# RWKV-7 recurrence on one core: outputs of the chunk behind in one burst with the solve

## The chip, the cores and the metric

The kernel runs on one NeuronCore of a Trainium2 chip. The metric is the device time of one execution in microseconds, as the median of several runs. TensorE (PE, with its weight loads PEld), VectorE (DVE), ScalarE (ACT), GpSimd (POOL) and SyncE (SP, which issues nearly all transfers) run side by side and wait for each other by semaphores.

## The reference

One layer of a hybrid trunk over 512 frames and 16 meta tokens, width 2048. After RMSNorm one projection of 8,320 columns feeds two groups. Group A (16 heads of 64) is an RWKV-7 recurrence, group B a gated convolution of width 3. Both are gated, joined, sent through one output projection, added to the residual and normalised. The recurrence is what the change touches:

```python
def step(S, inp):
    r_t, w_t, k_t, v_t, kk_t, b_t = inp
    sa = jnp.einsum('bhvk,bhk->bhv', S, kk_t)
    S = (S * w_t[:, :, None, :] - sa[..., None] * b_t[:, :, None, :]
         + v_t[..., None] * k_t[:, :, None, :])
    y_t = jnp.einsum('bhvk,bhk->bhv', S, r_t)
    return S, y_t
```

It runs over the 16 meta frames and then over 512 real ones; the head outputs `y` are normalised per head (mean and variance over 64), scaled, gated and projected. All inputs and the output are float32.

## The kernel before

The frames are worked on in chunks of 64 (`CH`): chunk 0 holds the meta tokens, chunks 1 to 8 the real frames (`NCH` = 9). The 16 heads are 8 pairs; a pair fills 128 partitions, one head in each half. `prepare` and `invert` run once per pair or two pairs and write, per chunk, the operands of the recurrence to DRAM: decayed r and k products, the triangular inverse (`O_X`), the values (`vd`) and the decayed b and k (`bd`).

Then `recur` goes through the chunks in order. For one chunk c it does this on PE, with small float32 matmuls, 64 by 64 (the update: 128 rows by 64):

- **rz** (L1102, 32 matmuls, 16 in chunk 0): state times the kk operand, plus the part from the values inside the chunk. ACT negates it into `pn` (L1110).
- **solve** (L1119, 16 matmuls): the inverse times `pn`, into the second half of the same two PSUM banks. ACT and DVE copy it into `uv` (L1122, L1123).
- **zs** (L1131, 16 matmuls): `bw` times `uv`, the update of the state, in the bank of tag `misc`; DVE adds it to the state `st` and multiplies by the decay (L1152, L1153).
- **zy** (L1141, 48 matmuls): the chunk's outputs, from the old state, `vn` and `uv`, half in the bank of tag `ser`, half in the first half of rz's first bank. `norm` (L1160 to L1194) normalises them on DVE, ACT and POOL, and stores them to `yd` some time later.

The profile counts two matmuls, each with a weight load, for each of these float32 matmuls.

PE's order is the order of the program (a manual schedule); the other engines' queues are ordered ahead of time by a planner with priorities (`ahead()` raises one). Between the steps `fill(ns)` issues matmuls of the big input projection (L353 and L368, tiles `ps_C`, `ps_h`, `ps_B`, `ps_gc` in this stretch) until their planned time has reached ns; the projection is one generator, so the amount of filler is fixed by the sum of the budgets: `p` 2900 after rz, `u` 2900 after the solve, `s` 4200 plus `mid` 1000 at the end of the chunk. The weights of this filler arrive as `wr` by SP's queue (L159, 512 KB each, three buffers) and are split by ACT (L151) and DVE (L152) into high and low parts (`w`, six buffers). A scheduled store (`later`) leaves when the filler's planned time has come.

`load_chunk` loads one 192 KB tile `ct` for each pair, `load_shared` loads `vn`, `uv` (its other half) and `bw`. All of these have two buffers. Pairs 0 to 3 of chunk c + 2 and the shared tiles are requested at the end of chunk c, pairs 4 to 7 of chunk c + 1 after rz of chunk c.

After the last chunk the rest of the projection runs, and then the output projection (L1383).

Of the kernel before, what the change touches and what calls it, by code (L numbers as in the profile page):

```python
# [9 lines left out]
F32 = mybir.dt.float32  # L10
# [3 lines left out]
ALU = mybir.AluOpType  # L14
# [4 lines left out]
P = 128  # L19
# [5 lines left out]
CH = 64  # L25
NCH = SEQ // CH + 1
LP = NCH * CH
NPAIR = 8
# [9 lines left out]
OPW = 6 * CH  # L38
O_AR, O_KK, O_BR, O_X = 0, 128, 256, 320
# [50 lines left out]
def hymba_kernel(ctx: ExitStack, tc: tile.TileContext, xt, xtok, front, w_in, w_out, pv, lup, cst, msk, gf, out):  # L90
    nc = tc.nc
# [91 lines left out]
    pi = ph1.enter_context(tc.tile_pool(name="pi", bufs=1, space=PSUM))  # L183
# [66 lines left out]
    o = 0  # L250
# [62 lines left out]
    with tc.issue_after(head):  # L313
        nc.vector.tensor_scalar(
            out=omm, in0=pvt[:, V_MU : V_MU + 33], scalar1=-1.0, scalar2=1.0, op0=ALU.mult, op1=ALU.add
# [299 lines left out]
    def fill(ns):  # L615
        while ns > 0:
            seen = len(ready)
            t = step()
            if t is None:
                return  # L620
            ns -= t
            if len(ready) > seen:
                ns += FW["evac"]
# [23 lines left out]
    def ahead():  # L647
        return tc.high_priority(offset=AHEAD)
# [409 lines left out]

    def load_chunk(ch, c, pairs, ops):
        for i in pairs:  # L1060
            t = ch.tile([P, OPW], F32, tag=f"ct{i}", name=f"ct{i}_{c}", bufs=2)
            nc.sync.dma_start(t, spot(i, 0, P, c, 1, 1, 0, OPW))
            ops[c, i] = t

    def load_shared(ch, c, ops):
        n = CH * NPAIR * CH
        vn = ch.tile([P, NPAIR, CH], F32, tag="vn", name=f"vn{c}", bufs=2)
        uv = ch.tile([P, 2, NPAIR, CH], F32, tag="uv", name=f"uv{c}", bufs=2)
        bw = ch.tile([P, NPAIR, 2, CH], F32, tag="bw", name=f"bw{c}", bufs=2)
        nc.sync.dma_start(vn, vd[2 * c * n : (2 * c + 2) * n].rearrange("(s j d) -> s j d", j=NPAIR, d=CH))  # L1070
        for h, hs, ho in heads:
            if c < NCH - 1:
                nc.sync.dma_start(
                    uv[ho, h], vd[(2 * c + h) * n : (2 * c + h + 1) * n].rearrange("(s j d) -> s j d", j=NPAIR, d=CH)
                )
                nc.sync.dma_start(
                    bw[hs].rearrange("p j h d -> p (j h d)"),
                    bass.AP(
                        tensor=bd.tensor, offset=bd.offset + (h * (NCH - 1) + c) * CH * NPAIR * P,
                        ap=[[NPAIR * P, CH], [1, NPAIR * P]],  # L1080
                    ),
                )
        ops[c] = vn, uv, bw


    def recur(ch):
        ops = {}
        for c in range(2):
            load_chunk(ch, c, range(NPAIR), ops)
            load_shared(ch, c, ops)  # L1090
        st = None
        for c in range(NCH):
            last = c == NCH - 1
            vn, uv, bw = ops[c]
            z = [pz.tile([P, 2, 4, CH], F32, tag="tz", name=f"rz{c}_{e}") for e in range(2)]
            for k in range(4):
                for part in range(0 if c else 1, 2):
                    for e in range(2):
                        t = ops[c, 2 * k + e]
                        o = O_KK if part else O_AR  # L1100
                        for h, hs, ho in heads:
                            nc.tensor.matmul(  # L1102
                                z[e][ho if e else hs, 0, k], t[hs, o : o + CH],
                                vn[hs, 4 * e + k] if part else st[hs, 4 * e + k],
                                start=(part == 0 or c == 0), stop=(part == 1),
                            )
            pn = ch.tile([P, 2, 4, CH], F32, tag="pn", name=f"pn{c}", bufs=2)
            with ahead():
                for e in range(2):
                    nc.scalar.activation(pn[:, e], z[e][:, 0], AF.Copy, scale=-1.0)  # L1110
            if c and not last:
                load_chunk(ch, c + 1, range(4, NPAIR), ops)
            fill(FW["p"])
            for k in range(4):
                for e in range(2):
                    t = ops[c, 2 * k + e]
                    for h, hs, ho in heads:
                        m = ho if e else hs
                        nc.tensor.matmul(z[e][hs, 1, k], t[m, O_X : O_X + CH], pn[m, e, k], start=True, stop=True)  # L1119
            with ahead():  # L1120
                for h, hs, ho in heads:
                    nc.scalar.copy(uv[hs, h, 0:4], z[0][hs, 1])  # L1122
                    nc.vector.tensor_copy(uv[hs, h, 4:8], z[1][hs, 1])  # L1123
            fill(FW["u"])
            if not last:
                zs = pi.tile([P, NPAIR, CH], F32, tag="misc", name=f"zs{c}")
                for k in range(4):
                    for e in range(2):
                        j = 4 * e + k
                        for h, hs, ho in heads:  # L1130
                            nc.tensor.matmul(zs[hs, j], bw[:, j, h], uv[:, h, j], start=True, stop=True)  # L1131
            if c:
                zy = (pi.tile([P, 4, CH], F32, tag="ser", name=f"zy{c}"), z[0][:, 0])
                for k in range(4):
                    for n in range(3):
                        for e in range(2):
                            t, j = ops[c, 2 * k + e], 4 * e + k
                            for h, hs, ho in heads:
                                o = (O_AR + CH, O_KK + CH, O_BR)[n]
                                x = (st[hs, j], vn[hs, j], uv[hs, h, j])[n]  # L1140
                                nc.tensor.matmul(  # L1141
                                    zy[e][hs if e else ho, k], t[hs, o : o + CH], x, start=(n == 0), stop=(n == 2)
                                )
            if c + 2 < NCH:
                load_chunk(ch, c + 2, range(0, 4), ops)
                load_shared(ch, c + 2, ops)
            if not last:
                new = ch.tile([P, NPAIR, CH], F32, tag="st", name=f"st{c}", bufs=2)
                scale = dd[:, c].unsqueeze(2).to_broadcast([P, NPAIR, CH])
                with ahead():  # L1150
                    if c:
                        nc.vector.tensor_tensor(out=new, in0=zs, in1=st, op=ALU.add)  # L1152
                    nc.vector.tensor_tensor(out=new, in0=new if c else zs, in1=scale, op=ALU.mult)  # L1153
                st = new
            if c:
                norm(ch, zy, c)
            fill(FW["s"] + FW["mid"])


    def norm(ch, zs, c):  # L1160
        nv = ch.tile([P, 4, NPAIR], F32, tag="nv", name=f"nv{c}", bufs=2)
        yc = ch.tile([P, NPAIR, CH], F32, tag="yc", name=f"yc{c}", bufs=2)
        yt = ch.tile([P, NPAIR * CH], F32, tag="yt", name=f"yt{c}", bufs=2)

        def spread(j):
            return nv[:, j].unsqueeze(2).to_broadcast([P, NPAIR, CH])

        for z, j in zip(zs, (slice(0, 4), slice(4, NPAIR))):
            nc.vector.tensor_reduce(out=nv[:, 0, j], in_=z, op=ALU.add, axis=AX.X)
            nc.vector.scalar_tensor_tensor(  # L1170
                out=yc[:, j], in0=spread(0)[:, j], scalar=-1.0 / CH, in1=z, op0=ALU.mult, op1=ALU.add
            )
        yq = yt.rearrange("p (j s) -> p j s", s=CH)
        nc.scalar.activation(yq, yc, AF.Square)
        nc.vector.tensor_reduce(out=nv[:, 1], in_=yq, op=ALU.add, axis=AX.X)
        nc.gpsimd.tensor_scalar(
            out=nv[:, 2], in0=nv[:, 1], scalar1=1.0 / CH, scalar2=LNX_EPS, op0=ALU.mult, op1=ALU.add
        )
        rsqrt(nv[:, 3], nv[:, 2])
        nc.vector.tensor_tensor(out=yc, in0=yc, in1=spread(3), op=ALU.mult)  # L1180
        nc.vector.transpose(yt, yc.rearrange("p j s -> p (j s)"))

        def put():
            for b in range(4):
                nc.sync.dma_start(
                    bass.AP(
                        tensor=yd.tensor,
                        offset=yd.offset + (b // 2) * NPAIR * CH * SEQ + (c - 1) * CH + 32 * (b % 2),
                        ap=[[SEQ, 32], [32 * SEQ, 2 * NPAIR], [1, 32]],
                    ),  # L1190
                    yt[32 * b : 32 * b + 32].rearrange("p (t s) -> p t s", s=32),
                )

        later(10500, put)  # L1194
# [497 lines left out]
```

## Time and profile before

| | us |
|---|---|
| median of 3 runs | 991.01 |
| lowest, highest | 990.09, 991.07 |
| profiled execution | 991.42 |
| span of its instructions | 989.6 |
| PE busy | 980.0 |
| PEld busy | 908.2 |
| DVE busy | 706.9 |
| ACT busy | 391.2 |
| POOL busy | 126.8 |

The recurrence lies between about 621 us (first rz) and 767 us (last normalisation begun). In the profile, times are from the span's start. L followed by a number is a line of the kernel before. In a row such as `670.98 0.66 ACT L1110 ACTIVATE pn<-rz ... x2 [1.11 <-PE rz L1102]` stand the start, the length, engine, line, operation, output and inputs, shapes, count, and in brackets how long the engine was idle before it and what ended that. The chain of waits gives the work that ended last, step by step: start, length, engine, tile, line and count. A row of a table of windows gives for each engine the busy time and the number of instructions, then the clock share, the share of the DMA engines and GB/s. A row of DMA queues gives packets, megabytes and the share of the 16 DMA engines' time; q1 carries the data, q8 and q14 carry instructions. The clock of TensorE was 0.999 of full speed over the span.

### The profile page before, as it was taken

To read this page: it belongs to the slowest core of one execution; us is meant where nothing else is said; L and a number is where in the kernel's file an instruction comes from. 1 tells how busy PE (TensorE), PEld (TensorE's weight loads), DVE (VectorE), ACT (ScalarE), POOL (GpSimd) and SP (SyncE) were. 2 spreads that over 40 slices of the span, in tenths; PEclk is the share of its full clock that TensorE was granted. 3 is DMA by queue.
4 is the path that set the end of the run, shared out by engine and by line. 5 is a ranking of instruction groups with operands and counts; after the bars stand their busy time and mean duration, and the time that the engine had idled before them with its cause. 6 is when DMAs were issued, how large, how long until landed. Compare 5 with 4: busy or idle time off the path is not lost.

```text
span 989.6 us, 23389 instructions
## 1 busy us (share of the span) xinstructions
PE 980.0 (99%) x9511; PEld 908.2 (92%) x9511; DVE 706.9 (71%) x1415; ACT 391.2 (40%) x730; POOL 126.8 (13%) x241
## 2 busy tenths in 40 slices
PE   9999999999999999999999999999999999999996
PEld 9999999999998999998999998889888898888885
DVE  7777966578775779653778654365756697997897
ACT  7553432343322534322434323232332335556464
POOL 0110302112010121010111010011211102001001
PEclk9999999999999999999999999999999999999999
DMA  9436577246674284853275856999896697797654
GB/s 339 143 91 150 144 199 167 86 128 148 157 179 165 91 195 116 209 153 114 86 181 124 203 143 193 277 252 260 223 264 171 179 289 187 187 320 180 160 128 170
DMA packets 205531, 176.89 MB, mean 179 GB/s; under 512 B 138544, under 2 KB 168048, under 8 KB 205040
## 3 DMA queue, kind: packets, MB, share of 16 engines
q1 hardware_dynamic: 202976, 166.76, 60.4%
q0 software_dynamic: 2304, 8.39, 4.9%
q8 instruction: 74, 1.21, 0.5%
q14 instruction: 33, 0.27, 0.1%
q10 hardware_dynamic: 144, 0.26, 0.1%
HBM read 139.02 MB, written 36.35 MB: 177 GB/s over the span
## 4 chain that ended last, share of the span: by engine, by line
PE 96%; DVE 2%; issue 1%; DMA 0%; ACT 0%; POOL 0%; POOLq 0%; DVEq 0%; ACTq 0%
PE ps_v L353 9%; PE ps_h L353 9%; PE ps_C L353 9%; PE ps_g L353 9%; PE ps_B L368 9%; PE ps_gc L368 9%; PE ps_k L353 8%; PE ps_r L353 8%; PE M L1383 7%; PE P L1383 3%; PE Q L1383 2%; PE g L755 2%; PE ps_k L368 1%; PE ps_r L368 1%; PE ps_lora L368 1%; PE zy L1141 1%
## 5 line engine op out<-in xcount | busy, mean ns | idle before, releaser
L151 ACT CAST w<-wr 128x512 fp32r<-128x512 f32 x252 | 154.1, 619 | 293.9 <-PE ps_C L353 47.4
L152 DVE TENSOR_TENSOR w<-wr,w 128x512 fp32r<-128x512 f32 x252 | 174.7, 704 | 121.0 <-ACT w L151 119.8
L353 PE MATMUL ps_v<-xh,w 128*128 128x256 f32 (+2 forms) x512 | 84.0, 284 | 0.0
L368 PE MATMUL ps_B<-xh,w 128*128 128x512 f32 x256 | 83.4, 394 | 0.0
L353 PE MATMUL ps_h<-xh,w 128*128 128x256 f32 (+2 forms) x512 | 81.6, 281 | 0.0
L353 PE MATMUL ps_g<-xh,w 128*128 128x256 f32 (+2 forms) x512 | 81.4, 281 | 0.0
L368 PE MATMUL ps_gc<-xh,w 128*128 128x512 f32 x256 | 81.1, 392 | 0.0
L353 PE MATMUL ps_C<-xh,w 128*128 128x256 f32 (+2 forms) x512 | 80.8, 280 | 0.0
L353 PEld LDWEIGHTS ps_v<-xh,w 128*128 128x128 f32 x512 | 73.9, 188 | 0.3
L353 PE MATMUL ps_k<-xh,w 128*128 128x256 f32 (+1 forms) x448 | 73.4, 285 | 0.0
L353 PE MATMUL ps_r<-xh,w 128*128 128x256 f32 (+1 forms) x448 | 72.5, 280 | 0.0
L353 PEld LDWEIGHTS ps_g<-xh,w 128*128 128x128 f32 x512 | 71.9, 189 | 0.6 <-issue 0.2
L353 PEld LDWEIGHTS ps_h<-xh,w 128*128 128x128 f32 x512 | 72.1, 189 | 0.3
L353 PEld LDWEIGHTS ps_C<-xh,w 128*128 128x128 f32 x512 | 71.8, 189 | 0.2
L353 PEld LDWEIGHTS ps_k<-xh,w 128*128 128x128 f32 x448 | 64.7, 188 | 0.4
L353 PEld LDWEIGHTS ps_r<-xh,w 128*128 128x128 f32 x448 | 63.5, 189 | 0.4 <-issue 0.2
L353 PE MATMUL ps_h<-xl,w 128*128 128x256 f32 x256 | 57.3, 281 | 0.0
L368 PEld LDWEIGHTS ps_gc<-xh,w 128*128 128x128 f32 x256 | 47.8, 188 | 10.0
L368 PEld LDWEIGHTS ps_B<-xh,w 128*128 128x128 f32 x256 | 47.9, 188 | 9.7
L353 PE MATMUL ps_C<-xl,w 128*128 128x256 f32 x256 | 56.2, 280 | 0.0
L353 PE MATMUL ps_v<-xl,w 128*128 128x256 f32 x256 | 55.8, 278 | 0.0
L353 PE MATMUL ps_g<-xl,w 128*128 128x256 f32 x256 | 55.4, 278 | 0.0
(383 smaller groups left out, 2143.5 us busy)
## 6 DMA issues: line engine op xcount, KB each, us to landing
wr<-in_w_in_dram SPq DMA_DIRECT2D x126, 512.0 KB
ct<-opd SPq DMA_DIRECT2D x72, 192.0 KB
wo<-in_w_out_dram SPq DMA_DIRECT2D x24, 512.0 KB
x<-in_w_out_dram POOLq DMA_DIRECT2D x16, 512.0 KB, 5.9
opd<-ar SPq DMA_DIRECT2D x8, 576.0 KB
opd<-gt SPq DMA_DIRECT2D x16, 288.0 KB
bd<-bt SPq DMA_DIRECT2D x64, 64.0 KB
bw<-bd SPq DMA_DIRECT2D x16, 256.0 KB
```

Source lines behind the costliest of these rows:

```text
L151: nc.scalar.copy(hi, rq)
L152: low[q] = eng.tensor_tensor(out=lo, in0=rq, in1=hi.bitcast(F32), op=ALU.subtract).ins
L353: nc.tensor.matmul(ps[r][:, 0 : b - a], ww[:, k * P : (k + 1) * P], xx[:, kt, a:b], start=(kt == 0 and n == 0), stop=(kt == KT - 1 and n = ...
L368: nc.tensor.matmul(ps[r], ww[:, w], xx[:, kt, a:b], start=(kt == 0 and n == 0), stop=(kt == KT - 1 and n == 2))
L755: nc.tensor.matmul(z[h][:, c - c0], bk[hs, c, h : h + 2, :].rearrange("p a s -> p (a s)"), ar[hs, c].rearrange("p a s -> p (a s)"), start= ...
L1141: nc.tensor.matmul(zy[e][hs if e else ho, k], t[hs, o : o + CH], x, start=(n == 0), stop=(n == 2))
L1383: nc.tensor.matmul(bank[s], left(prod, jj, m, s), w, start=(jj == 0 and n == 0), stop=(jj == 7 and n == 2))
```

## The change

- `outputs(c)` is a function of its own now. In chunks 2 to 8 the outputs of chunk c - 1 are computed between rz and the solve of chunk c, in place of the filler `p`; the last chunk computes its own outputs as well, after the filler `u`.
- The `p` filler of chunks 1 to 7 is added at the end of the chunk (`s` + `mid` + `p`).
- After the solve and the filler `u` stands the update of the state alone. It is written to the first halves of rz's banks and added to the state in two halves, and then multiplied by the decay in one operation.
- The outputs of chunks 1 to 7 use the banks of tags `ser` and `misc`; `norm` of chunk c - 1 follows the solve of chunk c.
- `ct` of pairs 0 to 3, `vn` and `uv` get a third buffer, since chunk c - 1 is still read in chunk c. Pairs 4 to 7 of chunk c + 1 are requested behind the solve of chunk c instead of behind rz.

```diff
-            t = ch.tile([P, OPW], F32, tag=f"ct{i}", name=f"ct{i}_{c}", bufs=2)
+            t = ch.tile([P, OPW], F32, tag=f"ct{i}", name=f"ct{i}_{c}", bufs=3 if i < 4 else 2)
...
-        vn = ch.tile([P, NPAIR, CH], F32, tag="vn", name=f"vn{c}", bufs=2)
-        uv = ch.tile([P, 2, NPAIR, CH], F32, tag="uv", name=f"uv{c}", bufs=2)
+        vn = ch.tile([P, NPAIR, CH], F32, tag="vn", name=f"vn{c}", bufs=3)
+        uv = ch.tile([P, 2, NPAIR, CH], F32, tag="uv", name=f"uv{c}", bufs=3)
...
-        st = None
+        st, states = None, {}
+
+        def outputs(c, zy=None):
+            vn, uv, bw = ops[c]
+            zy = zy or [pi.tile([P, 4, CH], F32, tag=tag, name=f"zy{c}_{tag}") for tag in ("ser", "misc")]
+            for k in range(4):
+                for n in range(3):
+                    for e in range(2):
+                        t, j = ops[c, 2 * k + e], 4 * e + k
+                        for h, hs, ho in heads:
+                            o = (O_AR + CH, O_KK + CH, O_BR)[n]
+                            x = (states[c][hs, j], vn[hs, j], uv[hs, h, j])[n]
+                            nc.tensor.matmul(
+                                zy[e][hs if e else ho, k], t[hs, o : o + CH], x, start=(n == 0), stop=(n == 2)
+                            )
+            return zy
...
-            if c and not last:
-                load_chunk(ch, c + 1, range(4, NPAIR), ops)
-            fill(FW["p"])
+            zy = outputs(c - 1) if c > 1 else fill(FW["p"])
...
+            if c and not last:
+                load_chunk(ch, c + 1, range(4, NPAIR), ops)
+            if zy:
+                norm(ch, zy, c - 1)
             fill(FW["u"])
-            if not last:
-                zs = pi.tile([P, NPAIR, CH], F32, tag="misc", name=f"zs{c}")
...
+            if last:
+                norm(ch, outputs(c, [z[e][:, 0] for e in range(2)]), c)
+                fill(FW["s"] + FW["mid"])
+                break
+            for k in range(4):
+                for e in range(2):
+                    j = 4 * e + k
+                    for h, hs, ho in heads:
+                        nc.tensor.matmul(z[e][hs, 0, k], bw[:, j, h], uv[:, h, j], start=True, stop=True)
             if c + 2 < NCH:
                 load_chunk(ch, c + 2, range(0, 4), ops)
                 load_shared(ch, c + 2, ops)
...
+            with ahead():
+                for e in range(2):
+                    part = slice(4 * e, 4 * e + 4)
                     if c:
-                        nc.vector.tensor_tensor(out=new, in0=zs, in1=st, op=ALU.add)
-                    nc.vector.tensor_tensor(out=new, in0=new if c else zs, in1=scale, op=ALU.mult)
-                st = new
-            if c:
-                norm(ch, zy, c)
-            fill(FW["s"] + FW["mid"])
+                        nc.vector.tensor_tensor(out=new[:, part], in0=z[e][:, 0], in1=st[:, part], op=ALU.add)
+                    else:
+                        nc.vector.tensor_tensor(out=new[:, part], in0=z[e][:, 0], in1=scale[:, part], op=ALU.mult)
+                if c:
+                    nc.vector.tensor_tensor(out=new, in0=new, in1=scale, op=ALU.mult)
+            st = new
+            states[c + 1] = st
+            fill(FW["s"] + FW["mid"] + (FW["p"] if c else 0))
```

More of the change, by code (lines that the diff above doesn't have):

```diff
@@ L1123, in recur @@
                     nc.vector.tensor_copy(uv[hs, h, 4:8], z[1][hs, 1])
+            if c and not last:
+                load_chunk(ch, c + 1, range(4, NPAIR), ops)
+            if zy:
+                norm(ch, zy, c - 1)
             fill(FW["u"])
-            if not last:
-                zs = pi.tile([P, NPAIR, CH], F32, tag="misc", name=f"zs{c}")
[L1127 to L1131, printed above, removed]
-            if c:
[L1133 to L1143, printed above, removed]
+            if last:
[7 more added lines that the diff above has]
+                        nc.tensor.matmul(z[e][hs, 0, k], bw[:, j, h], uv[:, h, j], start=True, stop=True)
             if c + 2 < NCH:
@@ L1146, in recur @@
                 load_shared(ch, c + 2, ops)
[L1147 to L1150, printed above, removed]
-                    if c:
-                        nc.vector.tensor_tensor(out=new, in0=zs, in1=st, op=ALU.add)
-                    nc.vector.tensor_tensor(out=new, in0=new if c else zs, in1=scale, op=ALU.mult)
-                st = new
-            if c:
-                norm(ch, zy, c)
-            fill(FW["s"] + FW["mid"])
+            new = ch.tile([P, NPAIR, CH], F32, tag="st", name=f"st{c}", bufs=2)
+            scale = dd[:, c].unsqueeze(2).to_broadcast([P, NPAIR, CH])
+            with ahead():
+                for e in range(2):
+                    part = slice(4 * e, 4 * e + 4)
+                    if c:
+                        nc.vector.tensor_tensor(out=new[:, part], in0=z[e][:, 0], in1=st[:, part], op=ALU.add)
[6 more added lines that the diff above has]
+            fill(FW["s"] + FW["mid"] + (FW["p"] if c else 0))
     def norm(ch, zs, c):
```

## The prediction

> **What bounds the kernel now.** I read the page first (span, busy shares, queues, chain), then the chain of waits and the stages inside the recurrence, then ACT, DVE and the DMA queues there.
>
> ```profile
> span 989.6 us, 23389 instructions
> PE 980.0 (99%) x9511; PEld 908.2 (92%) x9511; DVE 706.9 (71%) x1415; ACT 391.2 (40%) x730; POOL 126.8 (13%) x241
> q8 instruction: 74, 1.21, 0.5%
> 621.00:755.00 134.00, 133.72 (x2323) 118.81 (x2322) 75.50 (x138) 37.83 (x77) 20.98 (x22) 1.00 0.90 252
> ```
>
> TensorE sets the end: PE is busy for 980.0 of 989.6 us. In the window of the recurrence (columns: PE, PEld, DVE, ACT, POOL, clock, DMA share, GB/s) it is idle for 0.28 of 134 us, at clock 1.00. Projection matmuls fill every gap of the recurrence, so shorter latency alone is worth nothing. Only what PE itself spends counts, and any new wait of PE. The DMA engines are 0.90 busy there, near their own limit. The profiled execution took 991.42 us, 1.8 more than its span and 0.4 above the median of 991.01.
>
> One chunk in the chain of waits (start, length, what, count):
>
> ```profile
> 669.86 1.09 PE rz L1102 x64
> 670.95 3.35 PE ps_C L353 x27
> 674.30 0.62 PE rz L1119 x32
> 674.92 3.35 PE ps_C L353 x27
> 678.27 1.08 PE zs L1131 x32
> 679.35 0.20 PE zy L1141 x2
> ...
> 680.85 0.04 PE zy L1141 x2
> 680.91 1.63 PE ps_C L353 x12
> 682.54 4.17 PE ps_h L353 x36
> 686.72 1.09 PE rz L1102 x64
> ```
>
> From rz to rz the period is 16.86 us. Each start of a run of small matmuls costs something of its own. Matmuls of rz and of the solve (L1119) have one shape: 64 take 1.09 and 32 take 0.62, so one takes 0.47/32 = 0.0147 us and the entry into the burst 0.15. The outputs (zy, from 679.35 to 680.91) are 96 matmuls: 96 x 0.0147 = 1.41 in 1.56, so the step from zs (128 rows) to zy (64 rows) costs 0.15 as well. Filler without a burst before it goes at 4.17/36 = 0.116 each; 27 of them would take 3.14 and take 3.35 behind a burst, so the way back costs 0.2.
>
> **The change part by part.**
>
> *Bursts.* The matmuls and the filler are the same in number: fill asks 11,000 ns per chunk before and, over the loop, after. Chunks 2 to 8 run rz, outputs of the chunk behind and solve as one burst: seven times the solve's entry (0.15) and one way back to filler (0.2) go. At chunks 1 to 7 no zy follows zs: seven times 0.15. Sum: 7 x 0.35 + 7 x 0.15 = 3.5 us off PE. Outputs of chunk 8 stay a burst of their own.
>
> *Does the solve wait for pn?* The filler between rz and solve was its cover; now it is the outputs.
>
> ```profile
> 670.98 0.66 ACT L1110 ACTIVATE pn<-rz 128x256 f32<-128x256 f32 x2 [1.11 <-PE rz L1102]
> 679.40 0.69 DVE L1152 TENSOR_TENSOR st<-zs,st 128x512 f32<-128x512 f32 x1 [0.63 <-PE zs L1131]
> 680.13 0.69 DVE L1153 TENSOR_TENSOR st<-st,dd 128x512 f32<-128x512 f32 x1
> 691.82 1.14 ACT L151 CAST w<-wr 128x512 fp32r<-128x512 f32 x2 [3.32 <-DMA wr<-in_w_in_dram]
> 692.87 0.75 ACT L1122 COPY uv<-rz 64x256 f32<-64x256 f32 x2
> ```
>
> ```profile
> 691.16 0.62 PE rz L1119 x32
> ```
>
> Both pn copies end at 671.64, 0.69 after rz; the outputs take 1.41. So the wait is nothing as long as ACT is free, with 0.7 to spare where 3.4 us of filler stood. If ACT is not free, the rest is PE idle. The last rows show the danger: casts held up by a late weight transfer ran until 692.87, and the uv copies that were due when the solve ended (691.78) began 1.1 late, hidden by filler. I take nothing, and keep 0 to 2 for it.
>
> *State update.* Two adds on halves instead of one, some 0.1 to 0.2 us more on DVE. After zs now come 8.1 us of filler instead of 1.56 of outputs and 5.2; st took 1.4 us. Cost nothing; without the filler it would be the full 1.6. zs lands in rz's banks, which pn has left by then; norm starts later by some 8 us of filler, its next reader (the next outputs) being a chunk away. Cost nothing.
>
> *Transfers.* The bytes are the same. Loads of ct 4 to 7 for the next chunk moved behind the solve and now wait for the outputs in the burst; behind them on SP's queue stand the yd stores, the weight loads and the next chunk's loads. They have 3.1 + 1.2 + 8.7 = 13 us until rz needs them. The third buffers let ct 0 to 3, vn and uv start at that burst too instead of behind the update. Nothing is queued on POOL by the change, whose part in norm moves with it. Cost nothing on PE, from 0 to 2 by way of the late casts above.
>
> *Instructions.* Here lies what the burst may cost. PE and PEld make 19,022 instructions for 74 packets of q8 (16 KB each): 257 per packet, so PE's program arrives in blocks of 256. PE's only stop in the recurrence, in the chain of waits, with q8 before and in it:
>
> ```profile
> 748.31 5.80 PE ps_h L353 x48
> 754.11 0.60 PE rz L1102 x26
> 754.72 0.82 issue
> 755.53 0.81 PE rz L1102 x35
> ```
>
> Queues of two windows, 742.5 to 753.2 and 753.2 to 754.4:
>
> ```profile
> q1 hardware_dynamic: 2396, 2.60, 85.1%
> ```
>
> ```profile
> q1 hardware_dynamic: 76, 0.13, 29.7%
> q8 instruction: 1, 0.02, 5.2%
> ```
>
> For 10.7 us no packet came, then one, and 1.1 to 1.3 us after it PE went on. That is a stop for want of instructions. From the first burst (621.08) to the stop PE executed 2323 + 2322 instructions and 32 waits, 4,677 = 18 x 256 + 69. So a block starts 69 instructions after the first burst, and each 256 on. Counted back from the stop, blocks start near 670.33 and 720.60:
>
> ```profile
> 670.31:755.00 84.69, 84.41 (x1543) 76.33 (x1536) 50.32 (x94) 23.70 (x48) 14.86 (x16) 1.00 0.86 244
> ```
>
> (3,079, less some 30 still running at the edge, and 20 waits, for 12 x 256 = 3,072.) Their packets, in windows 670.3 to 674.3, 674.3 to 675.5, and 720.7 to 721.5, 721.5 to 722.6:
>
> ```profile
> q1 hardware_dynamic: 456, 1.12, 102.8%
> ```
>
> ```profile
> q1 hardware_dynamic: 315, 0.43, 101.6%
> q8 instruction: 1, 0.02, 5.5%
> ```
>
> ```profile
> q1 hardware_dynamic: 64, 0.17, 98.3%
> ```
>
> ```profile
> q1 hardware_dynamic: 68, 0.20, 75.8%
> q8 instruction: 1, 0.02, 5.4%
> ```
>
> So as PE begins one block, the next is asked for and its packet comes 1 to 4 us later among busy queues (at least 4.9 at the stop, whose block began in the burst that ended at 748.31). A packet takes about 1.0, and 1.3 more until PE runs. A block lasts 7 us with filler in it, which hides this. The largest burst so far, zs with zy, holds 256 instructions in 2.64 us.
>
> The new burst holds 192 matmuls, 384 instructions, in 0.15 + 192 x 0.0147 = 2.97 us: a block that lies wholly in it lasts 128 x 0.0147 = 1.9. With two instructions per matmul, four or five waits per chunk and the filler counts that fill's budget gives, the burst of chunk 2 begins 778 instructions after the first burst; a block starts 837 after it, 59 into the burst, the next 315 into it. For chunk 4 it is 77 and 333, for chunk 7 97 and 353. In chunks 3, 5, 6 and 8 the start that counts lies so (211 to 255) that filler and zs help, about 5 us and more. So three stops are due, each of delay + 1.0 + 1.3 - 1.9 = delay + 0.4. Bounds: delay 0, with an instruction queue of some depth running ahead, gives nothing; delay 4, 4.4. Which delay? By the DMA shares:
>
> ```profile
> 666.00:669.80 3.80, 3.80 (x34) 3.63 (x32) 2.73 (x5) 2.22 (x4) 0.97 (x2) 1.00 0.99 300
> 676.50:680.80 4.30, 4.30 (x144) 4.08 (x142) 2.48 (x4) 0.62 (x1) 0.00 (x0) 1.00 0.46 115
> 728.50:731.40 2.90, 2.90 (x132) 2.63 (x130) 2.75 (x5) 0.63 (x1) 0.00 (x0) 1.00 0.36 61
> ```
>
> The queues are full ahead of rz (0.99) and run dry (0.46, 0.36) just where the outputs are about to free buffers. After the change the outputs free them in the merged burst, so that is where the dry stretch should move. I take the short delay, 1.2: 3 x 1.6 = 4.8 us. The stop of 754.72 (0.8) goes, since its block then ends elsewhere.
>
> [...]
>
> Sum: 991.42 - 3.5 - 0.8 + 4.8 = 991.9 us.
>
> **The rivals.**
>
> *Instructions come in time* (faster): the bursts' 3.5 and the 0.8 stay, 991.42 - 4.3 = 987.1. For it: one stop in the whole recurrence is thin evidence, my count of instructions may be off by a few tens, and dry queues may deliver within 0.5 us. Against it: the count of 256 fits, and no packet quoted at a burst's block came in under 0.9 us. With two of three stops at 0.6 it would still be 988.3.
>
> *Instructions come late* (slower): the delay is as at 670.33 where queues were full. At 2.7, the middle of 1 and 4 and a little over, each stop costs 3.1: 991.42 - 4.3 + 9.3 = 996.4. From a delay of 1.6 at each stop (3 x 2.0 = 6.0, 993.1) it is slower than before by over 0.2%. For it: DMA 0.90 busy. Against it: the dry stretch.
>
> *pn is late* (slower only with the stops): a cast that waits for weights stands ahead of pn on ACT. One or two such, of 1.1 less 0.7 up to 2 us each, give 0.4 to 4 on the sum, 992.3 to 996. Against it, in the view of waits (total, times, longest), ACT stood ready and waited for rz eight times:
>
> ```profile
> ACT pn L1110 <- PE rz L1102: 14.4, 8, 4.1
> ```
>
> *Nothing gained*: entries and ways back are not a cost of switching but of matmuls that queue anyway. Then 991.4 + 4.8 - 0.8 = 995.4. Against it: L1119's 0.62 and rz's 1.09 split the same way in each chunk.
>
> **How the numbers follow.** 0.2% is 2.0 us, about what a measurement of this kernel can tell from no change: 989.0 to 993.0. Stops of 0.8 to 1.9 each, 989.5 to 992.9: 0.40, the likeliest, 991.9. Instructions in time or nearly: 0.30, 987 to 989. Late instructions, late pn or no gain: 0.30, 993 to 998; above 996 lies 0.1, under 987.0 little. Range 987.0 to 996.0.
>
> **What would show it.** PE's matmul lines keep their counts. The chain shows rz x64, zy and rz x32 of the solve without filler between, some 2.97 us, and no zy behind zs. A gap named issue, or a break in PE's rows, about 313 to 355 instructions into the bursts of chunks 2, 4 and 7, with a q8 packet just before its end, is the stop; none there, and the time near 987, proves the first rival. A solve that follows an ACT cast held by a weight transfer proves pn late. The prediction is wrong most likely in the delay, or in where blocks fall.

## The result, and the profile after

The change made the kernel slower: 999.22 us as the median (996.05 to 1000.95), against 990.98 of the kernel before on the same chip, a ratio of 1.0086 with a 95% interval of 1.0072 to 1.0100. The prediction was 991.9, and the result lies above its range. The execution that was profiled is the shortest of the four, 996.05; what the longer ones add is shown by a second profile further down.

Span and TensorE of the page, and the window of the recurrence (the same stretch and columns as before):

```profile
span 994.3 us, 23392 instructions
PE 977.5 (98%) x9511; PEld 907.8 (91%) x9511; DVE 706.2 (71%) x1423; ACT 391.4 (39%) x730; POOL 128.3 (13%) x241
621.00:755.00 134.00, 126.39 (x2153) 113.55 (x2144) 71.47 (x137) 37.40 (x75) 19.04 (x20) 0.99 0.86 246
```

TensorE has the same 9511 matmuls. It was idle for 0.28 us of this window before; now it is idle for 7.61 us. The chain of waits shows where, and what a burst is without a stop (chunk 3 first, then the ends of the bursts of chunks 2, 4 and 7; the runs of outputs are left out):

```profile
672.66 1.09 PE rz L1118 x64
...
675.15 0.47 PE rz L1133 x32
675.62 3.35 PE ps_C L353 x27
```

```profile
656.23 2.38 issue
658.61 0.21 PE zy_misc L1103
...
691.48 1.19 issue
692.67 0.58 PE rz L1133 x21
```

```profile
741.14 0.33 PE rz L1133 x19
741.47 4.04 issue
745.51 0.50 PE rz L1133 x13
746.01 4.14 PE ps_C L353 x21
750.16 0.71 PE ps_h L353 x6
```

The burst of chunk 3 takes 675.62 - 672.66 = 2.96 us: rz, the outputs and the solve (L1133), whose 32 matmuls now take 0.47 and not 0.62. In chunks 2, 4 and 7 a gap without any named releaser stands inside the burst. From matmul to matmul the three gaps are 2.59, 1.41 and 4.26 us, 8.26 in all. The instruction behind each is number 12,993, 14,273 and 16,065 of PE's matmuls, weight loads and waits, counted from 0; the stop of the kernel before lay at 16,577. All four leave 193 when divided by 256. They are starts of blocks, 317, 337 and 359 instructions into their bursts (the prediction had 315, 333 and 353).

In the stop of chunk 7, the block ahead of it began at 739.34. The data and instruction queues in 739.4 to 743.2 and in 743.2 to 744.4:

```profile
q1 hardware_dynamic: 601, 1.24, 95.6%
```

```profile
q1 hardware_dynamic: 319, 0.44, 101.0%
q8 instruction: 1, 0.02, 5.2%
```

For 3.9 us only data came; then the packet of instructions, and 2.27 us after its start PE went on, at 745.51. In chunks 2 and 4 the packet began 2.10 and 0.80 us after the block, and PE went on 2.38 and 2.48 after that.

The time adds up. From the first rz to the end of the outputs of chunk 8, bursts took 37.24 us in 27 pieces before and take 42.47 in 20 now. Without the stops (a gap of 1.04 before, 8.26 now) that is 36.20 and 34.21. What the filler takes beyond the rates of a pure run fell from 5.33 to 3.78, once the slow clock behind the longest stop, 1.54, is set apart. So the change saved 1.99 + 1.55 = 3.5 us, as meant, and 1.04 with the old stop, and paid 8.26 and 1.54: 989.6 - 3.5 - 1.0 + 8.3 + 1.5 = 994.9, 0.6 over the span of 994.3; the first rz began 0.6 earlier. (The expectations below have 3.6, with 0.97 counted for the old stop.)

### The profile page after: what moved, and what is told of

Read it like the earlier page. It is cut to its first block, busy times and chain, and to the rows that moved or that the text cites. A ratio compares the mean times of both kernels' runs of the same rounds, so it can differ in the third digit from the quotient of the medians.

```text
span 994.3 us, 23392 instructions
## 1 busy us (share of the span) xinstructions
PE 977.5 (98%) x9511; PEld 907.8 (91%) x9511; DVE 706.2 (71%) x1423; ACT 391.4 (39%) x730; POOL 128.3 (13%) x241
## 3 DMA queue, kind: packets, MB, share of 16 engines
q8 instruction: 74, 1.21, 0.5%
## 4 chain that ended last, share of the span: by engine, by line
PE 93%; DVE 3%; issue 2%; DMA 1%; ACT 0%; POOL 0%; POOLq 0%; SPq 0%; DVEq 0%; ACTq 0%
PE ps_v L353 9%; PE ps_h L353 9%; PE ps_g L353 9%; PE ps_B L368 9%; PE ps_gc L368 9%; PE ps_C L353 9%; PE ps_k L353 8%; PE ps_r L353 8%; PE M L1394 7%; PE P L1394 3%; PE Q L1394 2%; PE g L755 2%; PE ps_k L368 1%; PE ps_r L368 1%; PE ps_lora L368 1%
```

## The experiments

The theory: the bursts' gain is real, and blocks of 256 instructions that lie nearly wholly in a burst stop PE until the next packet has come; the packet's delay among the data is what was mis-sized. The rivals: the stops are waits for loads or buffers; pn, ACT or the loads' new order cost the time; every burst of 384 instructions stops somewhere, wherever blocks begin.

**Move the blocks.** The changed kernel, with 34 (first kernel) or 18 (second) small float32 matmuls of constants ahead of the first rz, 136 and 72 instructions:

```diff
+        pad = pi.tile([P, 512], F32, tag="misc", name="pad")
+        for n in range(34):
+            o = n % 8 * CH
+            nc.tensor.matmul(pad[0:CH, o : o + CH], cs[0:CH, 0:CH], cs[0:CH, 0:CH], start=True, stop=True)
```

> The changed kernel with 34 small matmuls more (136 of PE's instructions, into a bank that nobody reads) ahead of the first rz, so that every block of 256 instructions begins 136 instructions earlier in the bursts. Theory (PE stops because a block of instructions that lies wholly in a burst of 384 has to be fetched in 1.9 us): the block starts move from 61, 222, 81, 4, 219, 103 and 218 instructions into the bursts of chunks 2 to 8 to 181, 86, 201, 124, 83, 223 and 82, so the stops leave chunks 2, 4 and 7 and come at chunks 3, 6 and 8, at 5 as well if its packet is late; each 1 to 4 us; the pads themselves cost 1.0 us. Time 992 to 1004. Rival (the stops belong to what chunks 2, 4 and 7 do: their transfers, their place in the projection, a late pn): they stay in chunks 2, 4 and 7, and the time is that of the changed kernel plus 1, about 1000.

Measured: 997.01 (995.48 to 997.96), ratio 1.0053 with an interval of 1.0038 to 1.0068. The pad and the stops in its chain of waits:

```profile
620.44 4.05 PE pad L1095 x67
676.45 0.94 issue
710.24 1.10 issue
727.43 1.20 issue
761.35 1.28 issue
```

The stops are gone from chunks 2, 4 and 7 and stand in chunks 3, 5, 6 and 8, each at an instruction that leaves 193 when divided by 256. No load, buffer or wait was changed, so where a stop can stand is set by the count of instructions. The four gaps sum to 5.39, and the pads cost 3.9 us of PE: all of them read and write partitions 0 to 63, and they go at 4.05/67 = 0.060 us each, four times the 0.0147 of the bursts, whose matmuls alternate between the halves of the partitions.

> The same with 18 small matmuls (72 instructions). Theory of the instruction fetch: block starts at 245 (11 before the burst), 150, 9, 188, 147, 31 and 146 instructions into the bursts of chunks 2 to 8; from a block's request to its use there are 3.0 us or more everywhere instead of 2.2 at three places, so the stops shrink to 0 to 1 us each, 0 to 4 in all, and the time is 988 to 992 (991.4 - 4.3 + 0.5 for the pads + 0 to 4). Rival (stops belong to chunks 2, 4, 7, or the time is lost elsewhere): 997 to 1001 as the changed kernel.

Measured: 994.76 (989.83 to 996.40), 1.0028, interval 1.0013 to 1.0042. Blocks now start 245, 150, 265, 188, 147, 287 and 146 instructions into the bursts of chunks 2 to 8 (the one before 256 less). Stops in the profiled execution, which was the slowest of ten:

```profile
677.91 0.25 issue
727.87 1.89 issue
743.19 1.99 issue
```

The median lies 2.8 above the upper end of what was expected. By the rate above, 36 matmuls of pad cost some 2.2 us and not 0.5; the gaps of the three stops, 0.53, 2.27 and 2.21, sum to 5.0; and the clock falls behind the last (0.64 over 4.8 us). Chunk 7 stops, at 287. At 727.87 PE stopped in the filler behind the burst of chunk 6, at the end of a block that held the last 237 instructions of the burst and 19 of filler: a block with some filler in it stops PE too, when its packet is 3.03 us late. So what counts is not whether a block lies wholly in a burst, but the time that it lasts against delay + 2.3.

**Loads and buffers alone**, in the kernel before:

```diff
-            t = ch.tile([P, OPW], F32, tag=f"ct{i}", name=f"ct{i}_{c}", bufs=2)
+            t = ch.tile([P, OPW], F32, tag=f"ct{i}", name=f"ct{i}_{c}", bufs=3 if i < 4 else 2)
...
-        vn = ch.tile([P, NPAIR, CH], F32, tag="vn", name=f"vn{c}", bufs=2)
-        uv = ch.tile([P, 2, NPAIR, CH], F32, tag="uv", name=f"uv{c}", bufs=2)
+        vn = ch.tile([P, NPAIR, CH], F32, tag="vn", name=f"vn{c}", bufs=3)
+        uv = ch.tile([P, 2, NPAIR, CH], F32, tag="uv", name=f"uv{c}", bufs=3)
...
(load_chunk(ch, c + 1, range(4, NPAIR), ops) moved behind the solve)
```

> The kernel before with the change of the buffers and of the loads alone: third buffers for ct 0 to 3, vn and uv, and the request of ct 4 to 7 behind the solve; the bursts are as before. Theory of the instruction fetch: no burst over 256 instructions, so 990 to 992, the time of before. Rival (the late request of ct 4 to 7 or the other order on SP's queue is what slows the changed kernel, by late weights or late operands): 994 or more.

Measured: 991.45 against 991.15, ratio 1.0001, interval 0.9992 to 1.0011. This part of the change costs nothing, as the prediction said.

**Half of the outputs in each burst.** Pairs 4 to 7 between rz and the solve, pairs 0 to 3 behind zs, so that bursts hold 288 and 160 instructions:

```diff
-            zy = outputs(c - 1) if c > 1 else fill(FW["p"])
+            zy = outputs(c - 1, None, (2, 3)) if c > 1 else fill(FW["p"])
...
-            if zy:
-                norm(ch, zy, c - 1)
...
(behind zs:)
+            if zy:
+                norm(ch, outputs(c - 1, zy, (0, 1)), c - 1)
```

> The changed kernel with only half of the outputs of the chunk behind (pairs 4 to 7) between rz and the solve; the other half (pairs 0 to 3) follows the state update in the second burst. The first burst is 144 matmuls, 288 instructions instead of 384; the second 80 matmuls. Theory of the instruction fetch: filler lies in nearly every block again, so stops are gone or under 1.5 us in all; the step from zs to outputs comes back (7 x 0.15 = 1.0 us) and pn is covered by only 0.7 us of outputs, so up to 0.2 us of wait per chunk. Time 988 to 990.5. Rival (the merge itself costs, by late transfers, ACT or DVE order): 995 to 1000, little better than the changed kernel.

Measured: 994.70 (990.62 to 999.76), 1.0034, interval 1.0016 to 1.0052; a miss on the slow side. The profiled execution, 992.14, has one stop for instructions (0.90 in the chain) and a wait that the changed kernel's profiles do not have. Chain of waits, and PE's waits (total, times, longest):

```profile
648.64 7.42 DMA wr<-in_w_in_dram
...
656.16 0.62 ACT w L151
...
656.80 0.39 ACT pn L1126
...
657.24 0.96 PE rz L1133 x32
```

```profile
PE rz L1133 <- ACT pn L1126: 1.5, 1, 1.5
PE rz L1133 <- issue: 0.9, 1, 0.9
```

This is the prediction's rival of the late pn, as it was put: a weight transfer of 7.42 us holds a cast on ACT, pn stands behind it, and the solve waits 1.5 us. The outputs between rz and solve take only 0.7 us here; the 0.7 us more that the changed kernel has there would have covered about half of this wait. In the changed kernel's own two profiles no wait for pn is among PE's waits; the kernels with the filler dealt out, further down, have one each. Why the median is 2.6 above the profiled execution, this run cannot say.

**Emptier queues.** The changed kernel, with no loads for chunks 3 to 8; they work on chunk 2's tiles (the loads are left out, so the output is another):

```diff
+            if c > 2:
+                ops[c, i] = ops[2, i]
+                continue
...
+        if c > 2:
+            ops[c] = ops[2]
+            return
```

> The changed kernel, in which chunks 3 to 8 load nothing: they work on chunk 2's ct, vn, uv and bw, so the output is not the reference's and the loads of six chunks are left out. PE's instructions and their order are the same. Theory (the packet of instructions comes late because the data queues are full): the DMA share in the recurrence falls well under 0.9, the packets at the bursts of chunks 4 and 7 come within about 0.8 us of the block's start, and the stops there shrink from 1.41 and 4.26 us to at most 1 each; chunk 2 keeps a stop of 1 to 3. Median 991 to 994, against 996 to 1001 of the changed kernel itself. Rival (the delay is that of the fetch itself, whatever the queues carry): the stops at chunks 4 and 7 stay at 1.4 to 4.3 us and the median at 996 to 1001. Second rival (what was 8.26 us of stops was a wait for loads and not for instructions): no stops at all, and 987 to 989.

Measured: 991.13 (989.70 to 995.25), 1.0006, interval 0.9992 to 1.0020. Its window of the recurrence and its stops:

```profile
621.00:755.00 134.00, 130.24 (x2185) 117.45 (x2184) 72.64 (x140) 38.81 (x77) 18.53 (x20) 1.00 0.52 140
```

```profile
655.97 0.99 issue
689.93 1.00 issue
739.72 1.76 issue
```

The DMA share fell from 0.86 to 0.52, and the stops stand at the same three instructions but shrank from 2.59, 1.41 and 4.26 to gaps of 1.21, 1.22 and 1.98, 4.41 in all; the packets began 0.73, 0.54 and 1.50 us after their blocks. So they are not waits for loads, and nearly half of the 8.26 is what the data add. This compares the shortest execution of ten with the shortest of four; the medians, 991.13 here and 1000.45 for the changed kernel on the same chip (next run), put the part of the loads higher. The rest stays with the loads of six chunks gone: the stop is not only a matter of queues. The theory's bound of 1 for chunks 4 and 7 was too low, and so was its 0.8 for the packet of chunk 7.

**The changed kernel once more**, on that chip:

> The changed kernel, unaltered, once more and on the same chip as its variants. Theory: three stops at the same three instructions of PE (the blocks' starts in the bursts of chunks 2, 4 and 7), of other lengths than 2.59, 1.41 and 4.26, each the packet's delay plus about 0.4; where one is over 4 us, TensorE's clock falls below 0.7 for some 5 us behind it. Median 996 to 1001, and a spread of several us from run to run. Rival (the places depend on what the DMA queues carry at the time): stops at other chunks than 2, 4 and 7.

Measured: 1000.45 (995.76 to 1001.42), 1.0085, interval 1.0060 to 1.0110. This profile is of the longest execution, 1001.42:

```profile
656.75 3.40 issue
...
695.49 2.59 issue
...
746.86 4.04 issue
```

```profile
661.30:669.00 7.70, 7.70 (x52) 6.07 (x52) 4.97 (x11) 1.98 (x4) 1.88 (x2) 0.72 0.69 214
751.50:756.30 4.80, 4.80 (x33) 4.65 (x32) 1.86 (x4) 1.94 (x4) 1.27 (x2) 0.70 0.38 138
```

The same three instructions, with gaps of 3.62, 2.81 and 4.26: 10.69. Behind the first and the last the granted clock fell (0.72 and 0.70 in these windows), and the filler's excess is 7.05, 3.27 above the 3.78 without a slow clock. 989.6 - 3.5 - 1.0 + 10.7 + 3.3 = 999.1, against a span of 999.7. So most of the 5.4 us between the two profiled executions of this kernel comes from the stops (2.4) and the slow clock (1.7); the other runs have times alone.

**No burst over 256 instructions.** Outputs directly behind the solve, rz and zs alone with filler behind each:

```diff
-            zy = outputs(c - 1) if c > 1 else fill(FW["p"])
+            fill(FW["p"])
...
(behind the copies of uv:)
+            zy = outputs(c - 1) if c > 1 else None
...
-            fill(FW["s"] + FW["mid"] + (FW["p"] if c else 0))
+            fill(FW["s"] + FW["mid"])
```

> The outputs of the chunk behind directly after the solve instead of before it: rz stands alone with filler behind it, the solve and the outputs are one burst of 128 matmuls (256 instructions), zs stands alone with filler behind it. No burst holds a whole block of 256 instructions and more, and pn and uv have filler to hide in. Theory (blocks' starts in bursts over 256 instructions are what cost): no stop over about 1 us, one or two small ones as before had; of the bursts' gain only the step from zs to the outputs goes, 7 x 0.15 = 1.05 us. Median 989.5 to 991.5, ratio 0.999 to 1.001. Rival (the order itself, outputs ahead of state update and norm, costs time): 993 or more without stops.

Measured: 992.46 (990.78 to 993.88), 1.0018, interval 1.0009 to 1.0027. The profiled execution, 993.08, has three stops, gaps of 1.05, 0.68 and 0.71:

```profile
657.89 0.83 issue
692.61 0.46 issue
731.23 0.49 issue
```

Bursts without stops take 37.70 - 2.44 = 35.26, 0.9 less than before; the stops, 1.4 more than the old one, take it back, and the median lies 1.0 above the range that was expected. Splitting the burst is no cure as long as a block holds little filler: the one that ends at 657.89 held 41 instructions of rz, 28 of filler and 187 of the next burst. It lasted 5.3 us up to the stop, and its packet came 3.87 late.

**Deal the filler out by blocks.** The changed kernel, with budgets of filler moved between chunks so that a block starts 153 to 227 instructions into each burst; no matmul more or less:

```diff
+        fill(FW["shift"][0])
         st, states = None, {}
...
-            fill(FW["s"] + FW["mid"] + (FW["p"] if c else 0))
+            fill(FW["s"] + FW["mid"] + (FW["p"] if c else 0) + FW["shift"].get(c + 1, 0))
...
+    shift={0: 6930, 2: 550, 3: -3743, 4: 4293, 6: -3082, 7: 2202, 8: -1761},
```

> The changed kernel with its filler dealt out otherwise: 63 filler matmuls more ahead of the first rz, and ahead of the bursts of chunks 2 to 8 so many more or fewer (from 34 fewer to 39 more) that in each of the seven merged bursts of 384 instructions one block of 256 starts 153 to 227 instructions after the burst's start (227, 154, 227, 186, 153, 227, 152). Each block then has at least some 12 to 50 filler matmuls in it, 1.4 to 6 us, and none lies wholly in a burst. No matmul is added or left out. Theory (only blocks that lie nearly wholly in a burst stop PE): stops of 8.26 us in the changed kernel become at most 2 in all; 989.6 span less the bursts' gain of 3.6 and the old stop of 1.0 is a gain left of 2.5 to 4.5 us: median 986.5 to 989.0, ratio 0.995 to 0.998. Rival (a stop wherever a burst of 384 stands, the store being refilled late anyway): stops of 1 to 3 us at most bursts, median 993 to 1000. Second rival (the filler dealt out otherwise makes loads or weights late): PE waits for ct, vn or weights, and 990 to 994 without fetch stops.

Measured: 989.35 (987.96 to 991.28) against 990.66, ratio 0.9988, interval 0.9979 to 0.9996. That is 1.3 us below the kernel before: the interval leaves out 1, but the prediction takes 2.0 us for what a measurement can tell from no change; against the change, with the same merged bursts, it is about 1% (1.0085 there, each against the kernel before on its own chip). What is left, in PE's waits of the recurrence, on ACT, and in the chain at the burst of chunk 4:

```profile
PE ps_h L353 <- issue: 1.5, 1, 1.5
PE ps_C L353 <- issue: 1.3, 1, 1.3
```

```profile
697.80 0.72 ACT L487 ACTIVATE cv<-u,pvt 128x512 f32<-128x512 f32 x1 [2.38 <-POOL u L485]
698.54 0.66 ACT L1127 ACTIVATE pn<-rz 128x256 f32<-128x256 f32 x2
```

```profile
698.98 0.96 PE rz L1134 x32
```

The two stops lie in filler, behind the bursts of chunks 3 and 6, whose blocks start at some 153 (231 instructions of burst, then 25 of filler) and whose packets came 2.32 and 2.13 late; their gaps are 1.78 and 1.57. What the burst of chunk 4 lost, 0.53, is no stop for instructions: no block ends there, and the solve waited for pn. ACT stood at `cv`, an operation of the convolution that waited for POOL, and began pn when that was done, at 698.54; the solve could begin at 698.98. So the prediction's late pn comes in merged bursts too, here behind another operation than a cast. The expectation of at most 2 us of stops was missed by 1.4, and the time by 0.35: 986.5 to 989.0 was expected.

> As the kernel with its filler dealt out otherwise, by another deal: 93 filler matmuls more ahead of the first rz; blocks start 165, 220, 191, 184, 163, 219 and 162 instructions into the bursts of chunks 2 to 8, nearer the middle (192), at the price of larger moves of filler (up to 35 matmuls fewer ahead of a burst). Theory: stops of at most 1 us in all, 986.0 to 988.5, ratio 0.995 to 0.9975, and not slower than the other deal by over 1 us unless a load is late. Rival as there: 993 to 1000 with stops at most bursts; second rival, late loads (chunks 5, 6 and 8 follow the chunk before after 12 to 13 us instead of 17): a named wait of rz for ct or vn of 0.5 to 3 us and 989 to 993.

The second deal (`shift={0: 10780, 3: 3302, 4: -2202, 5: -3743, 6: -3853, 7: 3192, 8: -3302}`) was to do better and did not: 990.59 (988.02 to 993.18), 0.9998, interval 0.9989 to 1.0008. Its profile is of the slowest execution:

```profile
671.08 0.24 issue
729.25 3.28 issue
```

One packet, 4.7 us late, stops PE for 3.55 in the filler behind chunk 6, and the clock falls again. That block held the last 223 instructions of the burst and 33 of filler; it lasted 3.7 us, enough for a delay of 1.3 or so. No wait for loads is among PE's waits; the burst of chunk 8 lost another 0.5 to a pn that ACT began late, behind `cv` and a cast. So placing the blocks removed the stops in the bursts from both profiles, and not the long delay.

## Why the prediction was wrong

*The bursts' gain.* Predicted 3.5, measured 3.5; the burst 2.97, measured 2.96; solve without entry 0.47. Right. The rival that nothing is gained falls.

*The old stop.* It went, as said.

*Where the stops fall.* Predicted in chunks 2, 4 and 7 and nowhere else: right in both profiles of the change, within 6 instructions. That a stop moves with the count of instructions is shown by the two kernels with pads. That chunks 3, 6 and 8 are harmless held, with filler or zs in their blocks, as given. For chunk 5 it was luck. The prediction looked at the block that starts some 255 instructions into that burst; the block ahead of it starts at 4 and ends at 260, so it lies wholly in the burst, without filler, and by the prediction's own rule a stop was due. It ran through in 1.90 us. This is its row in the table of windows, and the only instruction packet of 705.45 to 706.3, just ahead of it:

```profile
706.30:708.20 1.90, 1.90 (x129) 1.90 (x132) 0.57 (x1) 0.66 (x2) 0.00 (x0) 1.00 0.00 0
```

```profile
q8 instruction: 1, 0.02, 8.4%
```

The packet began 0.8 us before PE began the block, while PE was in filler, and PE went on 2.7 us after it. In the second profile of the change it began 0.9 before. So a packet can begin before PE begins the block that it was counted from, and the delay can be below 0, which the prediction's bounds (0 to 4) left out. When a packet is asked for, and how far PE's queue runs ahead, no trace here shows.

*How long a stop is.* Here the step failed. The form, delay + 1.0 + 1.3 - 1.9, held: with the measured delays of 2.10, 0.80 and 3.90 it gives 2.5, 1.2 and 4.3, against 2.59, 1.41 and 4.26. The delay was taken as 1.2 each, because "that is where the dry stretch should move". It moved there only in chunk 4. The bursts of chunks 2, 4 and 7 in the table of windows (DMA share next to last):

```profile
653.74:658.61 4.87, 2.49 (x160) 2.35 (x159) 1.72 (x3) 1.78 (x4) 0.00 (x0) 1.00 0.93 333
688.88:692.67 3.79, 2.60 (x168) 2.50 (x169) 1.42 (x5) 0.66 (x2) 0.00 (x0) 1.00 0.61 173
738.60:745.51 6.91, 2.87 (x180) 2.74 (x180) 2.11 (x5) 1.05 (x3) 0.00 (x0) 1.00 0.97 321
```

Shares of 0.93, 0.61 and 0.97 stand beside stops of 2.59, 1.41 and 4.26. With the queues at 0.90 on average, the full delay, 2.7, was the better choice; it stood in the text as the rival that gave 996.4, and the shortest execution took 996.05. That this agrees so well is partly chance: the rival's stops are 9.3 where 8.26 was measured, and it has no term for the slow clock of 1.5 that follows. So the term of 4.8 was 8.26, and 10.69 in the other profile.

*What was not in the sum at all.* The filler behind the longest stop ran slow: 27 of them behind the stop of chunk 7 took 4.85 where the same number behind chunk 3 took 3.35, and the window after it shows the clock:

```profile
745.50:750.70 5.20, 5.19 (x40) 5.03 (x39) 1.86 (x4) 1.82 (x4) 1.25 (x2) 0.67 0.40 131
745.80:749.10 3.30, 3.30 (x24) 3.19 (x17) 1.68 (x4) 1.36 (x3) 0.00 (x0) 0.50 0.53 173
749.30:752.00 2.70, 2.70 (x47) 2.50 (x46) 0.68 (x2) 0.62 (x1) 1.84 (x2) 1.00 0.00 0
```

The 0.67 is a mean: the clock stands at 0.50 from 745.8 to 749.1, and at 1.00 from 749.3 on. That is 1.5 more here, and 3.3 where two stops were long. With 3.5 to 5.9 from the stops, this takes 991.9 to between 996.9 and 1001.1, and 996 to 1001 were measured. The clock fell behind the stops of 4.26, 3.62 and 3.55 us, but in the second kernel with pads behind one of 2.21 too (a mean of 0.64 over 4.8 us), while it stayed at 1.00 behind one of 2.27 in the same profile and one of 2.59 in the first profile of the change (windows of 5.0 us each), and one of 2.81 in the second brought no drop. So the length of a stop alone does not set it. What sets the clock back stays open.

*Wait for pn, state update, loads.* Nothing in the two profiles of the change, as taken, but for 0.3 us that the very first rz waited for `vn` in one of them. The late pn is real all the same: 1.5 us where half of the outputs cover it, and 0.5 us under the full cover in each kernel with the filler dealt out.

*Crossings of blocks.* In the first profile of the change they cost no stop where blocks hold filler or zs, as in chunks 3, 6 and 8, nor in chunk 5, where the packet came ahead of the block; where 256 instructions go in 1.9 us and the packet begins after the block, they cost 1.4 to 4.3 us each.

What stays open: what makes one packet wait 0.5 and another 4.7 us. Full data queues are a part, shown by the kernel without loads (gaps of 4.41 us in all at a DMA share of 0.52, against 8.26 at 0.86), but the packet of chunk 7 was still 1.50 late there. In one stop, that of chunk 4 in the second profile of the change, the packet began 0.71 after the block and PE went on 3.96 after it, so the stretch of 1.0 + 1.3 can be longer too. Whether the time can be had whole, by keeping transfers away from the blocks' starts, was not tried.

## What to carry to other kernels

Where many small matmuls stand in one burst, count instructions, weight loads included, before counting microseconds: here a block of 256 that was executed in less time than the next one needed until PE ran it (1.9 us against 3 to 6 us in the changed kernel's stops, with the data queues busy) stopped the engine, so filler between small matmuls can be worth more than the switches that it costs. Where the arrival of instructions is the limit, the place of the blocks is something to schedule: the same merged bursts cost 8 us, or nothing, or gained 1, by the deal of the filler alone. And when a stop's length hangs on a queue that is busy for nine tenths of the time, take the full queue's delay as the likeliest, and ask what clock the engine has after it.

## What was not expected of the hardware

- A packet of instructions came later where the queues carried more data: with the same TensorE instructions it began 2.10, 0.80 and 3.90 us after its block began with the loads of all chunks, and 0.73, 0.54 and 1.50 without those of six (DMA share of the recurrence 0.86 and 0.52). Where it began 0.8 us before its block, 256 instructions went in 1.90 us without a stop.
- PE went on 2.27 to 2.81 us after a packet began, in 22 of the 25 stops with a gap of 0.5 us or more that ten of the eleven profiles show, at a DMA share of 0.52 as at 0.86 to 0.90; in the other three after 3.09, 3.45 and 3.96.
- Behind the four stops of 3.55 to 4.26 us the granted clock was 0.67 to 0.72 on average over 4.8 to 7.7 us; once it was 0.64 over 4.8 us, behind a stop of 2.21. In the one of these stretches that is shown in finer windows it was 0.50 for 3.3 us (745.8 to 749.1), and then 1.00.
- Of the small float32 matmuls, counted as in the profile (two for each, 64 by 64), those of the pads, which all read and write partitions 0 to 63, took 0.060 us each (4.05/67), and those of rz and the solve, which alternate between the halves of the partitions, 0.0147.
